# A two-layer transformer trunk on one core: layer 1's modulation without unread columns, the second product in parts of 512 and 256, and the reciprocal square root as a GpSimd power

## The chip, the cores and the metric

The kernel runs on one core of one Trainium2 chip. The metric is the device time of one execution in microseconds (us), as the median of several runs. A core has five engines that work side by side and wait for each other through semaphores: TensorE (PE in the profile, with its weight loads as PEld), VectorE (DVE), ScalarE (ACT), GpSimd (POOL) and SyncE (SP), which issues most DMAs here.

## What is computed

The reference is a trunk of two layers over 512 latent tokens and 256 context tokens, of width 1024. Cut to what matters:

```python
for l in range(2):
    last = l == 1
    m_lat = silu(c) @ w_mod[l] + b_mod[l]          # 6 x 1024
    m_ctx = silu(c_ctx) @ w_mod[l] + b_mod[l]      # 6 x 1024
    sh1, sc1, ga1, sh2, sc2, ga2 = m_lat;  csh1, csc1, cga1, csh2, csc2, cga2 = m_ctx
    h_lat = rmsnorm(x_lat, norm1_g[l]) * (1 + sc1) + sh1
    h_ctx = rmsnorm(x_ctx, norm1_g[l]) * (1 + csc1) + csh1
    z_lat = h_lat @ w_in[l]                        # q, k, v, u, g
    z_ctx = h_ctx @ w_in[l]                        # in the last layer: k and v alone
    # q and k: rmsnorm per head, rotary;  attention over context and latent keys
    # g: gelu, layernorm per group of 128, mixed over 128 positions, times gelu(u)
    x_lat = x_lat + ga1 * (concat(attn_lat, gm_lat) @ w_out[l])
    x_lat = x_lat + ga2 * (relu(modulate(rmsnorm(x_lat), sh2, sc2) @ w_ff1[l]) ** 2 @ w_ff2[l])
    if not last:
        # the same for x_ctx with cga1, csh2, csc2, cga2
return x_lat
```

In the last layer the context gives keys and values and nothing more. Of the context's modulation it needs csh1 and csc1; cga1, csh2, csc2 and cga2 have no reader there.

## The kernel before, in words

Everything is float32. Each product is made of three matmuls on rounded halves: weights and activations are split into a high part `hi` (ScalarE, L207) and a rest `lo` (L208, VectorE or GpSimd), and hi*hi, hi*lo and lo*hi are added up in PSUM through `mm` (L203). A weight block of 128x1024 comes by DMA into `raw`, is split into a ring of four slots, and its slot is released when its last matmul is issued. Activations lie with the channels on the partitions: `X` holds 768 columns, latent tokens in 0 to 511 and context tokens in 512 to 767.

The order of instructions is set in two steps. The kernel's text is written by a planner (`Flow`) with a virtual clock: each matmul adds its cost (L204), and pieces of work are deferred by fixed delays (`PAR`) or drawn from "fillers". Then a scheduler orders each engine's instructions by priority and by its own model of their cost. In layer 0's feed-forward, chunks 0 to 6, VectorE and ScalarE keep the order of the text (`FM0`, L1052); elsewhere, past the start of the program, every engine is ordered by the scheduler. At run time each engine goes through its queue in order, so an instruction that waits holds up all behind it.

**The modulation.** For layer 0 it runs on TensorE (`mod_chunk`). For layer 1, `mod_wide` (L353) runs during layer 0's feed-forward on the engines that have time: 12 blocks j of 512 columns, 8 rows k each. For each k and each of the two conditions (0 latent, 1 context), ScalarE multiplies the weights by one value of silu (L371 for k = 0, L374 for the others) and GpSimd adds the product to `acc` (L375). VectorE then transposes and sums (L386, L387), PE makes a small product (L392), and `mod_store` (L395) adds the bias. The blocks are, two by two, sh1, sc1, ga1, sh2, sc2, ga2. The function yields nine times per block, and the feed-forward draws one step at a time through `more()` (L1013).

**The feed-forward.** `ff1` (L992) makes one tile of 128 hidden channels for all 768 columns, in two parts of 384 (`DENSE`, L538), and `relu2` (L957) squares it in four instructions (L960, L965, L966, L967). Every four tiles form a chunk, and the second product `proj4` (L792, called at L1040) adds a chunk's part to `X`: for 8 output tiles m and for the parts in `passes`, 12 matmuls and then `gate` (L785), which does X = X + ga2 * product (L790). A gate that crosses column 512 is cut there in two, since the two sides have different factors. The second product writes to double banks of PSUM (`pa`, two of them, a part in each half); for every third tile to one bank of `pb` and one of `pt`. In chunk 7 the parts of layer 0 are 512 and 256 in two separate passes already; layer 1 has only the 512 latent columns.

**The reciprocal square root.** `rsqrt` (L280) is a guess from the bits of the number (L283) and two refining steps (L286 to L293): nine small VectorE instructions. It is used by
- `Norm.sums` (L447): twice in layer 0's first norm, twice for each other norm; 4 or 2 columns. The norms of layer 1 are its first (at the end of layer 0's feed-forward) and its second. `diag` (L456) and a broadcast matmul (L460) follow.
- `qk` (L613), once per bank of queries (8 columns) or keys (4 columns). The result is multiplied in at L614, in layer 1 on GpSimd, which also does the sum before it at L608; then come the split (L619, L620) and the transposes on PE (`turn`, L632).
- `sink_g` (L725), once per bank of the gate, 4 columns; VectorE's L727 follows.

In layer 1's attention, `attn_tile` makes a score tile in one of two `pa` buffers; VectorE takes the row maximum (L831), ScalarE the exponential (L834).

Of the kernel before, what the change touches and what calls it, by code (L numbers as in the profile page):

```python
# [8 lines left out]
F32 = mybir.dt.float32  # L9
# [151 lines left out]
def trunk(ctx: ExitStack, tc: tile.TileContext, xT, pk1, pk2, rope, wsT, w_mod, w_tok, w_u, w_out, w_ff1, w_ff2, outT):  # L161
# [115 lines left out]
        state["freed"] += n  # L277
        fl.defer(PAR["REL"], settle)

    def rsqrt(v, n):  # L280

        yi = small(n, I32)
        vec.tensor_scalar(yi, v.bitcast(I32), -0.5, 1595932665.0, op0=ALU.mult, op1=ALU.add)  # L283
        y = yi.bitcast(F32)
        t, r = small(n), small(n)
        vec.tensor_tensor(out=t, in0=y, in1=y, op=ALU.mult)  # L286
        vec.scalar_tensor_tensor(out=t, in0=t, scalar=-0.703952253, in1=v, op0=ALU.mult, op1=ALU.mult)
        vec.scalar_tensor_tensor(out=y, in0=t, scalar=1.681914091, in1=y, op0=ALU.add, op1=ALU.mult)
        vec.tensor_tensor(out=t, in0=y, in1=y, op=ALU.mult)
        vec.tensor_tensor(out=r, in0=t, in1=v, op=ALU.mult)  # L290
        vec.tensor_scalar(t, r, 0.375, -1.25, op0=ALU.mult, op1=ALU.add)
        vec.tensor_tensor(out=t, in0=t, in1=r, op=ALU.mult)
        vec.scalar_tensor_tensor(out=y, in0=t, scalar=1.875, in1=y, op0=ALU.add, op1=ALU.mult)  # L293
        return y
# [5 lines left out]
    ident = P1("ident")  # L300
    ones = const.tile([128, 128], F32, name="ones")
    pool_e.memset(ones, 1.0)
    X = [unit(f"X{i}", [128, 2, T], F32) for i in range(4)]
    for i in range(4):
        nc.sync.dma_start(X[i][:, :, 0:SEQ], xT[i][:, :, 0:SEQ])
# [47 lines left out]
    def mod_wide(l):  # L353

        raw = tk([128, 2, 512], F32)

        def load(i):
            j, k = divmod(i, KT)
            if j < 12:
                (nc.gpsimd if PAR["MQ"] else nc.sync).dma_start(raw[:, k % 2, :], w_mod[l, j, k // 2][:, (k % 2) * 512:(k % 2) * 512 + 512])  # L360
        load(0)
        for j in range(12):
            acc = unit("C1", [128, 2, 512], F32)
            for k in range(KT):
                w = raw[:, k % 2, :]
                load(j * KT + k + 1)
                for cond in range(2):
                    a, s = acc[:, cond, :], sc[:, k, cond:cond + 1]
                    if cond in PAR["MP"]:
                        if k == 0:  # L370
                            act.activation(a, w, AF.Copy, scale=s)  # L371
                        else:
                            p = tsm([128, 512])
                            act.activation(p, w, AF.Copy, scale=s)  # L374
                            pool_e.tensor_tensor(out=a, in0=a, in1=p, op=ALU.add)  # L375
                    elif k == 0:
                        vec.tensor_scalar_mul(a, w, s)
                    else:
                        vec.scalar_tensor_tensor(out=a, in0=w, scalar=s, in1=a, op0=ALU.mult, op1=ALU.add)
                if k not in PAR["YK"]:  # L380
                    yield

            part = small(32).rearrange("p (c b) -> p c b", c=2)
            for cond in range(2):
                tr = tsm([128, 512])
                vec.transpose(tr, acc[:, cond, :])  # L386
                vec.tensor_reduce(out=part[:, cond, :], in_=tr.rearrange("p (b i) -> p b i", i=32), axis=AX.X, op=ALU.add)  # L387
                if cond in PAR["YC"]:
                    yield
            p4 = pt((128, 2, 4))  # L390
            for a in range(4):
                pe.matmul(p4[a * 32:a * 32 + 32], P1("sel"), part.rearrange("p c (m a) -> p c m a", a=4)[:, :, :, a], start=True, stop=True)  # L392
            mod_store(l, j, p4.rearrange("p b a -> p a b"))

    def mod_store(l, j, src):  # L395
        b0 = PK1["bmod"][0] + l * 48 + j * 4
        vec.tensor_tensor(out=modT[l][:, j * 4:j * 4 + 4, :], in0=src, in1=c1[:, b0:b0 + 4].unsqueeze(2).broadcast_to([128, 4, 2]), op=ALU.add)
        if j // 2 in (1, 4):
            w, k0 = (0 if j // 2 == 1 else 1), (j % 2) * 4
            g0 = PK1["ng"][0] + (l * 2 + w) * 8 + k0  # L400
            vec.scalar_tensor_tensor(out=Amod[l][w][:, k0:k0 + 4, :], in0=modT[l][:, j * 4:j * 4 + 4, :], scalar=1.0,
                                     in1=c1[:, g0:g0 + 4].unsqueeze(2).broadcast_to([128, 4, 2]), op0=ALU.add, op1=ALU.mult)

    cx = kv0 = None

# [12 lines left out]
    class Norm:  # L418
# [17 lines left out]
        def sums(self, *others):  # L436

            every = (self,) + others
            ps = pt()
            o = 0  # L440
            for a in every:
                for t in range(a.n // 128):
                    pe.matmul(ps[:, o:o + 1], a.acc[:, t * 128:(t + 1) * 128], ones[:, 0:1], start=True, stop=True)
                    o += 1
            v = small(o)
            vec.tensor_scalar(v, ps[:, 0:o], 1.0 / D, EPS, op0=ALU.mult, op1=ALU.add)
            r = rsqrt(v, o)  # L447
            o = 0
            for a in every:
                a.diag(r[:, o:o + a.n // 128])  # L450
                o += a.n // 128
# [130 lines left out]
    def layer(l, h, nxt, K, kv=None, kv0=0):  # L582
# [11 lines left out]
        def qk(ps4, tp, nh, which):  # L594

            sq = tsm([128, 2, nh, 64])
            act.activation(sq, ps4, AF.Square)
            ss = small(2 * nh)
            vec.tensor_reduce(out=ss.rearrange("p (a b) -> p a b", b=nh), in_=sq, axis=AX.X, op=ALU.add)
            t1 = tw([128, 2, nh, 64])  # L600
            if tp < 2:
                bcast = lambda a: a.unsqueeze(2).broadcast_to([128, 2, nh, a.shape[-1]])
                vec.tensor_tensor(out=t1, in0=ps4, in1=bcast(G[:, which, 0, tp * 2:tp * 2 + 2, :]), op=ALU.mult)
                t2 = tsm([128, 2, nh, 64])
                for hf in range(2):
                    o, i = slice(hf * 32, hf * 32 + 32), slice(32 - hf * 32, 64 - hf * 32)
                    vec.tensor_tensor(out=t2[:, :, :, o], in0=ps4[:, :, :, i], in1=bcast(G[:, which, 1, tp * 2:tp * 2 + 2, o]), op=ALU.mult)
                (pool_e if l in PAR['R1'] else vec).tensor_tensor(out=t1, in0=t1, in1=t2, op=ALU.add)  # L608
            else:
                g = P2(("qg", "kg")[which]).unsqueeze(1).unsqueeze(1).broadcast_to([128, 2, nh, 64])  # L610
                vec.tensor_tensor(out=t1, in0=ps4, in1=g, op=ALU.mult)
            vec.tensor_scalar(ss, ss, 1.0 / HD, EPS, op0=ALU.mult, op1=ALU.add)
            r = rsqrt(ss, 2 * nh)  # L613
            (pool_e if l in PAR['R2'] else vec).tensor_tensor(out=t1, in0=t1, in1=r.rearrange("p (a b) -> p a b", b=nh).unsqueeze(3).broadcast_to([128, 2, nh, 64]), op=ALU.mult)  # L614
            return t1

# [98 lines left out]
        def sink_g(gp):  # L715
            def f(tp, ps):
# [5 lines left out]
                    vec.bn_aggr(out=mv[:, i, :], in_=st[:, i, :])  # L722
                ve = small(4)
                vec.tensor_scalar(ve, mv[:, :, 1], 4 * EPS, None, op0=ALU.add)
                r = rsqrt(ve, 4)  # L725
                for i in range(4):
                    (pool_e if l in PAR['VG'] else vec).tensor_scalar(v[:, i * 128:i * 128 + 128], v[:, i * 128:i * 128 + 128], mv[:, i, 0:1], r[:, i:i + 1], op0=ALU.subtract, op1=ALU.mult)  # L727
                if len(mixes) > 1:
# [289 lines left out]
        def steady(chs):  # L1018
            for ch in chs:
                if ch < 7:  # L1020
                    ff1(ch * 4 + 4)
                    more()
                R = [H.pop(ch * 4 + kk) for kk in range(4)]
                end = ch == 7
                passes, post = [list(dense)], None
                if end and last:
                    post = lambda m, off: nc.sync.dma_start(outT[m], xk(m)[:, 0:SEQ])
                elif end:
                    more(96)
                    n1 = {p[0]: Norm(1, 0, *p) for p in ((0, 512, 0), (512, 256, 1))}  # L1030
                    passes = [[(0, 512)], [(512, 256)]]

                    def post(m, off):
                        nr = n1[off]
                        nr.step(m)
                        if m == 7:
                            if not nxt:
                                nxt.extend(unit(f"A{k}", [128, 2, T]) for k in range(8))
                            nr.finish_later(nxt, None if off == 0 else PAR["NC"])
                for n, _ in enumerate(proj4(("ff2", l, ch), R, 5, passes, "b" if end else "a", post)):  # L1040
                    fl.tick()
                    if n % 2 == 1 and not end:
                        more()
                if not end:
                    for i in range(1, 4):
                        ff1(ch * 4 + 4 + i)
                        more()
# [121 lines left out]
```

## Time and profile before

| | |
|---|---|
| median of 3 runs | 1515.79 us (1515.77 to 1517.52) |
| profiled execution | 1516.59 us |
| its span, first to last instruction | 1514.8 us |
| PE busy | 1463.9 us, 8804 matmuls |
| VectorE busy | 959.7 us, 1874 instructions |
| ScalarE busy | 682.4 us, 1142 instructions |
| GpSimd busy | 403.5 us, 362 instructions |
| mean granted TensorE clock | 0.995 |

How to read the lines that follow. A stretch (a row of the view by windows) gives start and end in us from the span's start, its length, then for PE, PEld, DVE, ACT and POOL the busy time and the number of instructions, then the granted TensorE clock (1.00 is full), the DMA share and GB/s. A group of instructions gives line, engine, operation, output <- inputs, shapes and count, then the total busy time in us and the mean in ns of one, then the idle time before them and what ended it. A timeline row gives start, length, engine, line and operation. A waits row gives who waited for whom: total, times, longest. A row of the chain gives start, length and what, in the chain of work that ended last. L207 is line 207 of the kernel.

Layer 0's attention and projections lie before about 345 us, its feed-forward between 370 and 890, layer 1's projections between 925 and 1040, its attention until 1145, its feed-forward from 1172 to the end.

### The profile page before, as it was taken

How to read it: one execution, taken by the hardware profiler on the slowest of the kernel's cores; microseconds unless marked ns; L12 is line 12 of the kernel's file. 1: busy time of each engine (PE TensorE's matmuls, PEld its weight loads, DVE VectorE, ACT ScalarE, POOL GpSimd, SP SyncE). 2: the span in 40 equal slices, each digit the busy share in tenths (PEclk: the TensorE clock that was granted, in tenths of full speed). 3: DMA queues.
4: the chain of work that ended last, by engine and by line, in shares of the span. 5: the costliest groups of instructions: out<-in, count | busy, mean ns of one | idle time of the engine just before them, and what ended most of it. 6: DMA issues, size and time to landing. Idle time of an engine off the chain costs nothing.

```text
span 1514.8 us, 22788 instructions
## 1 busy us (share of the span) xinstructions
PE 1463.9 (97%) x8804; PEld 1316.3 (87%) x8804; DVE 959.7 (63%) x1874; ACT 682.4 (45%) x1142; POOL 403.5 (27%) x362
## 2 busy tenths in 40 slices
PE   6999899999999999999999999998999999999998
PEld 2899687787899999999999988996899888888887
DVE  5877967787755455555555548888887644444443
ACT  3542455674445454544545334535784333322221
POOL 0112421312054555554545513044212000000000
PEclk9999999999999999999999999999999999999999
DMA  9221344401234333343434311321001323333332
GB/s 362 66 71 55 118 177 156 138 1 42 74 105 132 112 112 125 112 125 98 134 103 127 107 45 56 98 70 56 29 1 56 112 98 98 98 97 97 96 95 76
DMA packets 49948, 148.83 MB, mean 98 GB/s; under 512 B 5424, under 2 KB 6832, under 8 KB 49840
## 3 DMA queue, kind: packets, MB, share of 16 engines
q1 hardware_dynamic: 49264, 146.46, 30.2%
q8 instruction: 69, 1.13, 0.3%
q10 hardware_dynamic: 576, 0.92, 0.2%
q14 instruction: 39, 0.32, 0.1%
HBM read 145.26 MB, written 2.10 MB: 97 GB/s over the span
## 4 chain that ended last, share of the span: by engine, by line
PE 79%; DVE 12%; ACT 3%; DMA 3%; issue 1%; POOL 0%; SPq 0%; ACTq 0%; DVEq 0%; POOLq 0%
PE pa L203 51%; PE pb L203 20%; PE pt L203 3%; PE pt L850 3%; DVE lo L208 1%; PE pb L332 1%; ACT hi L207 1%; DMA raw<-in_w_tok 1%; DMA B<-in_w_mod 1%; DMA A<-in_w_mod 1%; DVE m L283 1%; DVE B L967 1%; DVE m L831 1%; ACT w L834 1%; DVE A L853 1%
## 5 line engine op out<-in xcount | busy, mean ns | idle before, releaser
L203 PE MATMUL pa<-A,hi 128*128 128x384 f32 (+2 forms) x1696 | 449.1, 347 | 1.9 <-ACT w L960 0.6
L207 ACT CAST hi<-raw 128x1024 fp32r<-128x1024 f32 x171 | 179.5, 1050 | 408.9 <-PE pa L203 325.9
L208 DVE TENSOR_TENSOR lo<-raw,hi 128x1024 fp32r<-128x1024 f32 x155 | 203.3, 1312 | 216.5 <-ACT hi L207 213.1
L203 PEld LDWEIGHTS pa<-A,hi 128*128 128x128 f32 x1696 | 304.7, 188 | 26.0 <-ACT w L960 1.8
L375 POOL TENSOR_TENSOR C<-C,s 128x512 f32<-128x512 f32 x168 | 240.4, 1462 | 244.7 <-ACT s L374 244.7
L203 PE MATMUL pa<-A,lo 128*128 128x384 f32 (+2 forms) x848 | 293.6, 347 | 1.1 <-DVE lo L208 1.1
L203 PE MATMUL pa<-B,hi 128*128 128x384 f32 (+1 forms) x900 | 246.5, 356 | 4.4 <-DVE X L790 4.4
L203 PEld LDWEIGHTS pa<-B,hi 128*128 128x128 f32 x900 | 162.9, 188 | 21.6 <-DVE X L790 9.4
L790 DVE SCALAR_TENSOR_TENSOR X<-pa,modT,X 128x384 f32<-128x384 f32 (+1 forms) x168 | 88.0, 547 | 141.9 <-PE pa L203 141.7
L203 PEld LDWEIGHTS pa<-A,lo 128*128 128x128 f32 x848 | 159.3, 188 | 12.3 <-DVE lo L208 1.5
L203 PE MATMUL pa<-B,lo 128*128 128x384 f32 (+1 forms) x450 | 158.1, 353 | 0.0
L203 PE MATMUL pb<-B,hi 128*128 128x256 f32 (+2 forms) x600 | 152.8, 341 | 0.4 <-DVE X L790 0.4
L374 ACT ACTIVATE s<-k,silu 128x512 f32<-128x512 f32 x168 | 114.3, 716 | 47.1 <-DMA k<-in_w_mod 27.6
L203 PE MATMUL pb<-hi,A 128*128 128x256 f32 x672 | 126.2, 285 | 0.0
L203 PEld LDWEIGHTS pb<-B,hi 128*128 128x128 f32 x600 | 103.9, 189 | 11.4 <-DVE X L790 1.0
L790 DVE SCALAR_TENSOR_TENSOR X<-pb,modT,X 128x512 f32<-128x512 f32 (+3 forms) x116 | 69.0, 602 | 69.0 <-PE pb L203 68.8
L203 PEld LDWEIGHTS pb<-hi,A 128*128 128x128 f32 x672 | 106.1, 191 | 0.2 <-issue 0.2
L203 PE MATMUL pb<-B,lo 128*128 128x256 f32 (+2 forms) x300 | 101.6, 339 | 0.0
L203 PE MATMUL pb<-lo,A 128*128 128x256 f32 x336 | 95.3, 284 | 0.0
L203 PEld LDWEIGHTS pa<-B,lo 128*128 128x128 f32 x450 | 84.4, 188 | 5.9
L434 POOL TENSOR_TENSOR acc<-acc,s 128x256 f32<-128x256 f32 (+1 forms) x43 | 47.0, 1092 | 138.7 <-ACT s L432 138.2
L834 ACT ACTIVATE w<-pa,m 128x768 f32<-128x768 f32 (+1 forms) x80 | 65.7, 821 | 38.2 <-DVE m L831 29.8
(171 smaller groups left out, 2321.9 us busy)
## 6 DMA issues: line engine op xcount, KB each, us to landing
raw<-in_w_ff SPq DMA_DIRECT2D x128, 512.0 KB, 3.5
k<-in_w_mod SPq DMA_DIRECT2D x96, 256.0 KB, 2.9
raw<-in_w_tok SPq DMA_DIRECT2D x19, 512.0 KB, 3.6
raw<-in_w_out SPq DMA_DIRECT2D x16, 512.0 KB, 3.5
lo<-in_w_mod SPq DMA_DIRECT2D x16, 512.0 KB, 4.5
hi<-in_w_mod SPq DMA_DIRECT2D x16, 512.0 KB, 3.7
A<-in_w_mod SPq DMA_DIRECT2D x8, 512.0 KB, 10.0
raw<-in_w_u SPq DMA_DIRECT2D x8, 512.0 KB, 3.6
```

What stands on the lines that cost most here:

```text
L203: pe.matmul(out, a, b, start=start, stop=stop)
L207: act.copy(hi, src)
L208: (eng or vec).tensor_tensor(out=lo, in0=src, in1=hi.bitcast(F32), op=ALU.subtract)
L283: vec.tensor_scalar(yi, v.bitcast(I32), -0.5, 1595932665.0, op0=ALU.mult, op1=ALU.add)
L332: pe.matmul(ps[q:q + 32, :], S32[:, k, :], ws_[k2 // 2][:, k2 % 2 * 512:(k2 % 2 + 1) * 512], start=k < ns, stop=k >= KT - ns)
L374: act.activation(p, w, AF.Copy, scale=s)
L375: pool_e.tensor_tensor(out=a, in0=a, in1=p, op=ALU.add)
L434: eng.tensor_tensor(out=self.acc, in0=self.acc, in1=sq, op=ALU.add)
L790: vec.scalar_tensor_tensor(out=xs, in0=src[:, s - off:e - off], scalar=modT[l][:, i * 8 + m, cond:cond + 1], in1=xs, op0=ALU.mult, op1=ALU ...
L831: vec.tensor_reduce(out=nmx, in_=ps[:, 0:nk], axis=AX.X, op=ALU.max, negate=True)
L834: act.activation(p, ps[:, 0:nk], AF.Exp, bias=nmx, accum_out=sm)
L850: pe.transpose(tp_[:, (kt - k0) * 128:(kt - k0) * 128 + 128], p[:, kt * 128:kt * 128 + 128], ident)
```

## The change

Three things, independent of each other.

1. `mod_wide`: for blocks j = 4 to 11 of layer 1 the context condition is left out, from ScalarE's products to the last store. One more `yield` keeps the number of steps per block at nine.
2. `steady`: the second product of layer 0, chunks 0 to 6, goes over the parts (0, 512) and (512, 256) in one pass, in place of (0, 384) and (384, 384). `ff1` keeps its parts of 384.
3. `rsqrt`: in layer 1 the nine VectorE instructions become one GpSimd instruction that raises the number to the power -0.5, with the exponents in a constant tile of 8 columns that GpSimd fills at the start. Layer 0 keeps the nine.

The diff, cut to its core:

```diff
-    def rsqrt(v, n):
-
+    def rsqrt(v, n, l=0):
+
+        if l:
+            y = small(n)
+            pool_e.tensor_tensor(out=y, in0=v, in1=mhalf[:, 0:n], op=ALU.pow)
+            return y
         yi = small(n, I32)
...
+    mhalf = const.tile([128, 8], F32, name="mhalf")
+    pool_e.memset(mhalf, -0.5)
...
         for j in range(12):
+            conds = range(2 if j < 4 else 1)
             acc = unit("C1", [128, 2, 512], F32)
...
-                for cond in range(2):
+                for cond in conds:
...
+            nc_ = len(conds)
             part = small(32).rearrange("p (c b) -> p c b", c=2)
-            for cond in range(2):
+            for cond in conds:
...
-                pe.matmul(p4[a * 32:a * 32 + 32], P1("sel"), part.rearrange("p c (m a) -> p c m a", a=4)[:, :, :, a], start=True, stop=True)
-            mod_store(l, j, p4.rearrange("p b a -> p a b"))
+                pe.matmul(p4[a * 32:a * 32 + 32, 0:nc_], P1("sel"), part.rearrange("p c (m a) -> p c m a", a=4)[:, 0:nc_, :, a], start=True, stop=True)
+            mod_store(l, j, p4[:, 0:nc_].rearrange("p b a -> p a b"), nc_)
+            if nc_ == 1:
+                yield
...
-            r = rsqrt(v, o)
+            r = rsqrt(v, o, self.l)
...
-            r = rsqrt(ss, 2 * nh)
+            r = rsqrt(ss, 2 * nh, l)
...
-                r = rsqrt(ve, 4)
+                r = rsqrt(ve, 4, l)
...
-                passes, post = [list(dense)], None
+                passes, post = [list(dense) if last else [(0, SEQ), (SEQ, CTX)]], None
```

`mod_store` takes the number of conditions and writes and reads only those columns.

More of the change, by code (lines that the diff above doesn't have):

```diff
@@ L391, in mod_wide, with mod_store @@
             for a in range(4):
-                pe.matmul(p4[a * 32:a * 32 + 32], P1("sel"), part.rearrange("p c (m a) -> p c m a", a=4)[:, :, :, a], start=True, stop=True)
-            mod_store(l, j, p4.rearrange("p b a -> p a b"))
-    def mod_store(l, j, src):
+                pe.matmul(p4[a * 32:a * 32 + 32, 0:nc_], P1("sel"), part.rearrange("p c (m a) -> p c m a", a=4)[:, 0:nc_, :, a], start=True, stop=True)
+            mod_store(l, j, p4[:, 0:nc_].rearrange("p b a -> p a b"), nc_)
+            if nc_ == 1:
+                yield
+    def mod_store(l, j, src, nc_=2):
         b0 = PK1["bmod"][0] + l * 48 + j * 4
-        vec.tensor_tensor(out=modT[l][:, j * 4:j * 4 + 4, :], in0=src, in1=c1[:, b0:b0 + 4].unsqueeze(2).broadcast_to([128, 4, 2]), op=ALU.add)
+        vec.tensor_tensor(out=modT[l][:, j * 4:j * 4 + 4, 0:nc_], in0=src, in1=c1[:, b0:b0 + 4].unsqueeze(2).broadcast_to([128, 4, nc_]), op=ALU.add)
         if j // 2 in (1, 4):
@@ L400, in mod_store @@
             g0 = PK1["ng"][0] + (l * 2 + w) * 8 + k0
-            vec.scalar_tensor_tensor(out=Amod[l][w][:, k0:k0 + 4, :], in0=modT[l][:, j * 4:j * 4 + 4, :], scalar=1.0,
-                                     in1=c1[:, g0:g0 + 4].unsqueeze(2).broadcast_to([128, 4, 2]), op0=ALU.add, op1=ALU.mult)
+            vec.scalar_tensor_tensor(out=Amod[l][w][:, k0:k0 + 4, 0:nc_], in0=modT[l][:, j * 4:j * 4 + 4, 0:nc_], scalar=1.0,
+                                     in1=c1[:, g0:g0 + 4].unsqueeze(2).broadcast_to([128, 4, nc_]), op0=ALU.add, op1=ALU.mult)
     cx = kv0 = None
```

## The prediction

> **What bounds the kernel now.** I read the busy table first, then the busy time by stretches, then the waits and the timelines inside the stretches where TensorE is not full.
>
> ```profile
> PE 1463.9 (97%) x8804; PEld 1316.3 (87%) x8804; DVE 959.7 (63%) x1874; ACT 682.4 (45%) x1142; POOL 403.5 (27%) x362
> ```
>
> TensorE (PE) has work 97% of the span. So a step pays only if it makes matmuls shorter or takes away some of the remaining idle time. The stretches tell where that idle time lies (columns: busy time and count of PE, weight loads, VectorE, ScalarE, GpSimd; then the granted clock).
>
> ```profile
> 370.00:878.00 508.00, 502.84 (x2916) 487.83 (x2915) 285.05 (x400) 241.70 (x330) 245.11 (x171) 1.00 0.36 112
> 878.00:985.00 107.00, 105.90 (x668) 95.48 (x667) 77.76 (x196) 47.97 (x79) 18.25 (x17) 1.00 0.21 65
> 985.00:1040.00 55.00, 47.98 (x364) 45.04 (x363) 49.58 (x127) 20.35 (x32) 27.70 (x18) 0.99 0.22 68
> 1145.00:1172.00 27.00, 25.36 (x196) 23.87 (x196) 23.46 (x61) 13.57 (x29) 6.65 (x6) 1.00 0.27 79
> ```
>
> The first row is layer 0's feed-forward, with the second product and layer 1's modulation in it: PE idles 508.00 - 502.84 = 5.2 us. The second is the turn to layer 1 and most of its input projections: 1.1 us idle. The third is the end of those projections and the first attention scores: 55.00 - 47.98 = 7.0 us idle, with VectorE (DVE) busy 90% of it. The fourth is layer 1's second norm: 1.6 us. The change touches these four and nothing else, so idle time of 14.9 us is nearly all that is to be had.
>
> **Part 1, layer 1's modulation.** For blocks j = 4 to 11 the context column goes. Per block that is one scaled copy and 7 scaled products on ScalarE, 7 additions on GpSimd, one transpose and one reduction on VectorE; over 8 blocks 64, 56 and 16 instructions.
>
> ```profile
> L375 POOL TENSOR_TENSOR C<-C,s 128x512 f32<-128x512 f32 x168 | 240.4, 1462 | 244.7 <-ACT s L374 244.7
> L374 ACT ACTIVATE s<-k,silu 128x512 f32<-128x512 f32 x168 | 114.3, 716 | 47.1 <-DMA k<-in_w_mod 27.6
> ```
>
> GpSimd loses 56 x 1.462 = 82 us, ScalarE 64 x 0.716 = 46 us. The loads stay, and so do the nine steps per block (seven rows, one transpose, one closing step), so everything else is issued where it was. All of it lies in the first stretch beside a PE that is 99% busy, where GpSimd was itself waiting 244.7 us for ScalarE: its direct worth is 0. One indirect effect is visible at the start of each second product:
>
> ```profile
> 557.90 1.92 DVE L967 TENSOR_TENSOR B<-w,B 128x768 fp32r<-128x768 f32 x1
> 559.74 0.61 DVE L790 SCALAR_TENSOR_TENSOR X<-pa,modT,X 128x384 f32<-128x384 f32 x1
> ```
>
> ```profile
> L967 DVE TENSOR_TENSOR B<-w,B 128x768 fp32r<-128x768 f32 x24 | 36.6, 1527 | 0.8
> PE pa L203 <- DVE X L790: 4.4, 5, 1.3
> ```
>
> PE waits for the first gated addition L790 (five times, 4.4 us in all), which stands in VectorE's queue behind a subtraction that took 1.92 us here and 1.527 on average. Halved GpSimd work should catch it less often. Bounds 0 and -1.0 us; I take -0.5.
>
> **Part 2, the second product in parts 512 and 256.** Layer 0, chunks 0 to 6, 8 tiles each: 56 tiles, 24 matmuls each, as before. Three rows of the chain, twelve matmuls each, with 384, 512 and 256 columns:
>
> ```profile
> 442.19 2.08 PE pt L203 x12
> 1195.08 2.72 PE pb L203 x12
> 299.37 1.43 PE pb L203 x12
> ```
>
> Before: 2 x 2.08 = 4.16 us a tile; after: 2.72 + 1.43 = 4.15. Over 56 tiles that is -0.6 us, the rounding of the rows. I call it 0. The gated additions change, because the boundary at column 512 no longer cuts a part in two:
>
> ```profile
> L790 DVE SCALAR_TENSOR_TENSOR X<-pa,modT,X 128x384 f32<-128x384 f32 x42 | 25.7, 613 | 13.1 <-PE pa L203 12.9
> L790 DVE SCALAR_TENSOR_TENSOR X<-pa,modT,X 128x128 f32<-128x128 f32 x42 | 14.7, 351 | 83.6 <-PE pa L203 83.6
> L790 DVE SCALAR_TENSOR_TENSOR X<-pa,modT,X 128x256 f32<-128x256 f32 x42 | 19.9, 475 | 0.0
> L790 DVE SCALAR_TENSOR_TENSOR X<-pa,modT,X 128x512 f32<-128x512 f32 x42 | 31.5, 750 | 45.2 <-PE pa L203 45.2
> ```
>
> Before 613 + 351 + 475 = 1439 ns a tile, after 750 + 475 = 1225: 56 x 0.214 = 12 us less on VectorE, which has half of this stretch free, so none of it counts. What counts is the wait at the start of a product. VectorE begins the first L790 when L967 is done, whatever PE does; PE reaches the wait 2.72 - 2.08 = 0.64 us later, and the longer addition ends 0.750 - 0.613 = 0.14 later. Each of the five waits shrinks by 0.5 us: -2.5 us if PE is given as many other matmuls ahead of the wait as now, and if it is given fewer, nothing. A bad order could cost one 0.14 at each of the seven starts, +1.0. I take -2.0.
>
> **Part 3, the power.** There are 34 reciprocal square roots, of nine VectorE instructions each; by the code 15 are layer 1's (four norms, seven query and key banks, four gate banks). Those 135 instructions go, and 15 GpSimd powers on 2 to 8 columns come. The stretch 985 to 1040 holds six of them (count of the first and last of the nine in it):
>
> ```profile
> L283 DVE TENSOR_SCALAR m<-m 128x8 int32<-128x8 int32 (+1 forms) x6 | 6.4, 1067 | 0.1
> L286 DVE TENSOR_TENSOR m<-m 128x8 f32<-128x8 f32 (+1 forms) x6 | 4.3, 708 | 0.2
> L287 DVE SCALAR_TENSOR_TENSOR m<-m,m 128x8 f32<-128x8 f32 (+1 forms) x6 | 3.1, 517 | 0.2
> L293 DVE SCALAR_TENSOR_TENSOR m<-m,m 128x8 f32<-128x8 f32 (+1 forms) x6 | 1.0, 163 | 0.1
> ```
>
> Undisturbed, one takes 0.163 us (the last row, which I take for the five others too). The first three take far more. So VectorE gives 6.4 + 4.3 + 3.1 + 6 x 1.0 = 19.8 us to them in a stretch where it is 90% busy. The timelines of VectorE and of GpSimd show why:
>
> ```profile
> 1030.18 2.32 DVE L283 TENSOR_SCALAR m<-m 128x8 int32<-128x8 int32 x1
> 1032.54 1.22 DVE L286 TENSOR_TENSOR m<-m 128x8 f32<-128x8 f32 x1
> 1033.79 2.27 DVE L287 SCALAR_TENSOR_TENSOR m<-m,m 128x8 f32<-128x8 f32 x1
> 1036.10 0.17 DVE L288 SCALAR_TENSOR_TENSOR m<-m,m 128x8 f32<-128x8 f32 x1
> 1036.58 0.95 DVE L831 TENSOR_REDUCE m<-pa 128x1 f32<-128x768 f32 x1
> ```
>
> ```profile
> 1030.07 2.40 POOL L208 TENSOR_TENSOR lo<-raw,hi 128x1024 fp32r<-128x1024 f32 x1
> 1032.42 1.30 POOL L608 TENSOR_TENSOR w<-w,s 128x512 f32<-128x512 f32 x1
> 1033.67 2.36 POOL L208 TENSOR_TENSOR lo<-raw,hi 128x1024 fp32r<-128x1024 f32 x1
> 1039.16 1.04 POOL L614 TENSOR_TENSOR w<-w,m 128x512 f32<-128x512 f32 x1 [3.12 <-DVE m L836]
> ```
>
> Each of the three tiny instructions ends just after a GpSimd instruction does; VectorE stood still for 5.8 us. Behind them in its queue is L831, the row maximum of the first score tile. ScalarE's exponential waits for that, and PE's third score tile waits for the exponential, since there are two score buffers:
>
> ```profile
> PE pa L203 <- ACT w L834: 4.3, 1, 4.3
> PE pt L632 <- DVE k L620: 1.8, 1, 1.8
> ```
>
> ```profile
> 1038.60:1042.00 3.40, 3.39 (x9) 2.78 (x10) 2.94 (x7) 1.93 (x3) 1.46 (x3) 0.53 0.09 37
> ```
>
> The pause of 4.3 us is followed by 3.4 us at a clock of 0.53, which loses another 3.4 x 0.47 = 1.6 us. [...]
>
> With the nine gone, L831 can follow the scaling L612 at about 1030.2, some six microseconds earlier than now, and the subtraction L620 that made PE wait 1.8 us follows directly on its ScalarE copy. At most 4.3 + 1.6 + 1.8 = 7.7 us come back. Against that stands the power itself, which the trace does not show.
>
> ```profile
> L208 POOL TENSOR_TENSOR lo<-raw,hi 128x1024 fp32r<-128x1024 f32 x16 | 39.6, 2480 | 13.7 <-ACT hi L207 13.6
> L839 POOL COPY rc<-m 128x64 f32<-128x64 f32 x80 | 19.2, 241 | 166.9 <-DVE m L836 154.3 <-PE pt L850 6.8 <-PE pb L871 3.2
> ```
>
> From below it costs 0.24 us, the copy, which handles more columns; from above 2.48, the longest two-input instruction. It is a series of steps per column on few columns, so I take 1.0 us, nearer to the copy. In the stretch six powers make 6 us, and GpSimd has 55.0 - 27.7 = 27.3 free. Queued behind each power are the product L614, or for a gate bank nothing; VectorE waits for gate-bank powers ahead of L727, and a subtraction of 2.4 us may stand ahead of a power in GpSimd's queue. The chain of a query bank gets shorter (nine instructions at 0.163 and their gaps, 1.7 us, become 1.0). Next late are that queue and the tail of VectorE's other work; I give back 1.7 of the 7.7 and take -6.0, with bounds -7.7 and 0.
>
> The four norms hold a similar chain ahead of a broadcast matmul, in stretches with 1.1 + 1.6 = 2.7 us of idle. There the power may stand behind an accumulation on GpSimd. Bounds: -2.7, and +3.0 if each of four powers costs 2.48 against 1.7. I take -0.5.
>
> **Sum.** -0.5 - 2.0 - 6.0 - 0.5 = -9.0 us. The profiled execution took 1516.59 us (its span of 1514.8 and 1.8 around it): 1507.6. The median of the runs shown, 1515.79, is 0.8 lower, which gives 1506.8. The lower bounds of the four terms add to -13.9 (1501.9). As the forecast's upper end I set -3.0 (1512.8), where the moved wait below begins; the upper bounds of the terms together, 0 + 1.0 + 0 + 3.0 = +4.0, belong to the rivals.
>
> **The rivals.** *The wait moves.* Powers of 2 to 4 us, or powers stuck behind GpSimd's 2.4 us subtractions, make PE wait for a turned bank or VectorE for L727. For it: GpSimd's queue is in order, and from 1030 to 1036 it is full. Against: from 1036.04 to 1039.16 it idles. Price: part 3 shrinks to nothing, leaving -2.5 us, 1513.3.
>
> *The power is slow, and GpSimd becomes the bound.* Its free 27.3 us are filled by six powers of 4.5 us; that is the point. At 6 us the stretch needs 27.7 + 36 = 63.7 us of GpSimd against 55 now, +8.7, and the four norms add up to 4 x (6 - 1.7) = 17, of which other matmuls cover perhaps half: with -2.5 from the feed-forward about +15, 1531. VectorE would be stopped as well, as by L208 above, 36 us against the 19.8 freed. [...] Against: no GpSimd row quoted here is longer than 2.5 us, even with 1024 columns.
>
> *The product's parts change nothing.* PE then reaches the wait with fewer other matmuls: part 2 is 0, 1508.8. It lies inside my forecast.
>
> That the change does not do what it says I exclude: no context tile of layer 1 reads the columns dropped.
>
> **How the numbers follow.** Forecast 0.70, the moved wait 0.17, the slow power 0.13. A measurement of this kernel can tell about 0.2%, 3.0 us. The forecast lies beyond that bound, the moved wait within it, the slow power on the other side: 0.70, 0.17, 0.13. The forecast's own range is 1501.9 to 1512.8; for eight in ten I go from 1501.5 to 1517.5, which takes in the moved wait and the mildest slow power.
>
> **What would show it.** Right: in the first stretch the same number of matmuls, PE's wait for L790 near 2 us; between 985 and 1040 no pause of 4 us ahead of a score matmul and no row with half the clock after it; 15 GpSimd powers near 1 us; 19 instead of 34 rows for each of the nine. Wrong: powers beyond 2.5 us, PE waiting for L614's bank or VectorE for a power, or new idle time in layer 1's attention, where the order of the work may come out differently.

## The result, and the profile after

The changed kernel takes 1510.24 us (median of 6 runs, 1507.94 to 1510.43) against 1517.53 us of the kernel before (6 runs, 1515.77 to 1520.26). The ratio is 0.9947, with a 95% interval of 0.9936 to 0.9957: 8 us faster, where 9 were forecast. Behind a ratio, here and below, a difference in us is the ratio applied to the about 1517 us that the kernel before took beside it. The profiled execution took 1510.43 us, its span 1508.6. The stretches of the prediction's first table, now (same columns):

```profile
370.00:878.00 508.00, 503.66 (x2940) 462.68 (x2938) 262.95 (x332) 200.57 (x267) 169.55 (x115) 1.00 0.35 112
878.00:985.00 107.00, 105.56 (x664) 95.36 (x664) 70.44 (x133) 49.05 (x80) 25.75 (x25) 1.00 0.22 69
985.00:1040.00 55.00, 52.60 (x392) 49.06 (x392) 35.74 (x78) 24.64 (x41) 37.93 (x27) 1.00 0.19 59
1145.00:1172.00 27.00, 25.29 (x186) 23.79 (x185) 21.38 (x49) 13.94 (x31) 4.17 (x6) 0.94 0.20 62
```

The third row is the step that counted. PE's idle time there is 55.00 - 52.60 = 2.4 us, down from 7.0; VectorE's busy time fell from 49.6 to 35.7 us, GpSimd's rose from 27.7 to 37.9, and the clock is full. The last row shows something new, a clock of 0.94. PE's longest wait between layer 0's last ReLU and the second norm, and the groups of the new instruction (L284 in this kernel):

```profile
PE pb L203 <- POOL A L791: 2.4, 2, 2.1
```

```profile
L284 POOL TENSOR_TENSOR m<-m,mhalf 128x4 f32<-128x4 f32 x8 | 8.7, 1088 | 39.3 <-DVE m L734 33.3 <-DVE m L456 3.7 <-DVE m L622 2.3
L284 POOL TENSOR_TENSOR m<-m,mhalf 128x8 f32<-128x8 f32 x4 | 7.0, 1760 | 0.0
L284 POOL TENSOR_TENSOR m<-m,mhalf 128x2 f32<-128x2 f32 x3 | 2.1, 711 | 9.1 <-DVE m L456 9.1
```

In layer 0's feed-forward PE still waits for the first gated addition (L800 in this kernel), 3.6 us in four waits where it was 4.4 in five:

```profile
PE pa L203 <- DVE X L800: 3.6, 4, 0.9
```

The waits of 4.3 us (a score matmul for the exponential) and 1.8 us (a transpose for the subtraction) are gone. The one that is now longest stands behind GpSimd's gate subtractions, L781 in the old numbering and L791 in the new. The powers take 0.71, 1.09 and 1.76 us for 2, 4 and 8 columns, (8.7 + 7.0 + 2.1) / 15 = 1.19 on average.

For a comparison free of shifts I cut each trace at four landmarks: layer 0's first and last ReLU, layer 1's last exponential, layer 1's first and last ReLU. Stage lengths in us, from one profile of each kernel:

| kernel | feed-forward 0 | to last exponential | to first ReLU | feed-forward 1 |
|---|---|---|---|---|
| before | 511.6 | 236.5 | 37.2 | 325.5 |
| after | 508.9 | 229.9 | 37.4 | 327.2 |
| part 1 alone (p1_mod) | 509.4 | 236.7 | 36.9 | 325.5 |
| part 2 alone (p2_parts) | 509.6 | 237.5 | 36.9 | 325.6 |
| 256 first (p2_small_first) | 520.6 | 237.3 | 36.9 | 325.6 |
| part 3 alone (p3_power) | 511.6 | 231.0 | 37.4 | 325.7 |
| power in the banks (p3_proj) | 511.4 | 231.0 | 36.9 | 325.6 |
| power in the norms (p3_norm) | 511.1 | 236.5 | 37.5 | 325.7 |
| subtractions on VectorE (wp_vec) | 511.4 | 230.4 | 36.9 | 325.5 |
| all, powers twice (all_twice) | 508.8 | 239.2 | 38.0 | 327.9 |

The change took 2.7 us from the first stage and 6.5 from the second, and gave 0.3 and 1.6 back in the last two. The time ahead of the first ReLU was 1.1 us longer in the profile after. From the unrounded lengths -2.7 - 6.5 + 0.3 + 1.6 = -7.3, and +1.1 makes the -6.2 by which the two spans differ. That first stretch is scatter: in every profile of this document PE, VectorE, ScalarE and GpSimd run the same instructions there in the same order, but for the one GpSimd instruction that fills the exponents, and yet it took 378.3 to 383.0 us. Layer 0's feed-forward, where parts 1 and 2 are left out and its code is as before (p3_power, p3_proj, p3_norm, wp_vec), differs from before by 0.5 us at most.

### The profile page after: what moved, and what is told of

Same layout as the page of the kernel before. It is cut to its first block, busy times and chain, and to the rows that moved or that the text cites. A ratio compares the mean times of both kernels' runs of the same rounds, so it can differ in the third digit from the quotient of the medians.

```text
span 1508.6 us, 22398 instructions
## 1 busy us (share of the span) xinstructions
PE 1461.8 (97%) x8804; PEld 1289.5 (85%) x8804; DVE 908.6 (60%) x1667; ACT 641.0 (42%) x1078; POOL 342.1 (23%) x322
## 4 chain that ended last, share of the span: by engine, by line
PE 83%; DVE 8%; ACT 3%; DMA 2%; POOL 2%; issue 2%; SPq 0%; POOLq 0%; ACTq 0%; DVEq 0%
PE pa L203 52%; PE pb L203 23%; PE pt L860 3%; PE pt L203 2%; PE pb L338 1%; POOL acc L444 1%; DMA raw<-in_w_tok 1%; DMA B<-in_w_mod 1%; PE pt L642 1%; DMA A<-in_w_mod 1%; DVE A L863 1%; DVE m L841 1%; DVE B L977 1%; ACT w L844 1%; PE pb L881 0%
## 5 line engine op out<-in xcount | busy, mean ns | idle before, releaser
L208 DVE TENSOR_TENSOR lo<-raw,hi 128x1024 fp32r<-128x1024 f32 x155 | 196.9, 1270 | 230.7 <-ACT hi L207 227.3
L203 PE MATMUL pa<-B,hi 128*128 128x512 f32 (+1 forms) x900 | 239.8, 355 | 3.6 <-DVE X L800 3.6
L382 POOL TENSOR_TENSOR C<-C,s 128x512 f32<-128x512 f32 x112 | 164.9, 1489 | 314.6 <-ACT s L381 272.6
L203 PEld LDWEIGHTS pa<-B,hi 128*128 128x128 f32 x900 | 158.8, 189 | 31.6 <-DVE X L800 5.9
L800 DVE SCALAR_TENSOR_TENSOR X<-pa,modT,X 128x512 f32<-128x512 f32 x126 | 82.9, 660 | 140.9 <-PE pa L203 140.9
L203 PE MATMUL pb<-B,hi 128*128 128x512 f32 (+1 forms) x600 | 156.9, 350 | 0.9 <-DVE X L800 0.9
L203 PE MATMUL pa<-B,lo 128*128 128x512 f32 (+1 forms) x450 | 157.7, 355 | 0.0
L800 DVE SCALAR_TENSOR_TENSOR X<-pb,modT,X 128x512 f32<-128x512 f32 (+3 forms) x116 | 70.8, 618 | 81.8 <-PE pb L203 81.6
L203 PE MATMUL pb<-B,lo 128*128 128x512 f32 (+1 forms) x300 | 104.5, 348 | 0.0
L381 ACT ACTIVATE s<-k,silu 128x512 f32<-128x512 f32 x112 | 76.9, 715 | 38.8 <-DMA k<-in_w_mod 25.9
L203 PE MATMUL pb<-A,hi 128*128 128x512 f32 (+2 forms) x288 | 81.7, 360 | 2.4 <-POOL A L791 2.4
```

The lines of the kernel that those rows point to most:

```text
L203: pe.matmul(out, a, b, start=start, stop=stop)
L208: (eng or vec).tensor_tensor(out=lo, in0=src, in1=hi.bitcast(F32), op=ALU.subtract)
L800: vec.scalar_tensor_tensor(out=xs, in0=src[:, s - off:e - off], scalar=modT[l][:, i * 8 + m, cond:cond + 1], in1=xs, op0=ALU.mult, op1=ALU ...
```

## Experiments: which part gave what

My theory was the prediction's: part 2 shortens PE's wait at the start of each product, part 1 adds little, and part 3 frees VectorE's queue at the end of the projections. The rivals: the feed-forward's gain is part 1's, or the whole is a lucky order of the work.

**Part 1 alone.** `rsqrt` and the product's parts as before:

```diff
+            conds = range(2 if j < 4 else 1)
...
-                for cond in range(2):
+                for cond in conds:
```

> The first part alone (modulation without the unread columns; products in 384 and 384, nine VectorE instructions everywhere). Of the 6.2 us between the two profiled spans, layer 0's feed-forward (first to last ReLU) gave 2.7. My theory (the gain there is the longer first part of the product): this one gives 0 to -1 us, 1515 to 1517, and the waits for the first gated addition stay at 4 to 5.3 us in all. Rival (halved GpSimd work stops slowing VectorE): all of the 2.7 us, 1513 to 1514.5, with the subtraction after ReLU below its 1527 ns mean.

Ratio 0.9989 (0.9980 to 0.9997), -1.7 us; the feed-forward's stage is 2.1 us shorter. PE's waits for the gated addition (L794 here) in that stage:

```profile
PE pa L203 <- DVE X L794: 2.6, 3, 0.9
PEld pa L203 <- DVE X L794: 7.1, 25, 1.3
```

Three waits instead of five: those at 698 and 767 us, of 1.3 and 0.6 us, are gone. Both signs failed: my theory had 4 to 5.3 us of waits, and the rival's shorter subtraction has a mean of 1484 ns, hardly under 1527. The traces show two different causes. At 698 us the subtraction was caught before: a GpSimd addition that had begun ahead of it ran from 695.26 to 697.08 us, and the subtraction took 1.94 us and ended 0.82 after it. With part 1 alone it took 0.96; first before, then part 1 alone:

```profile
695.96 1.94 DVE L967 TENSOR_TENSOR B<-w,B 128x768 fp32r<-128x768 f32 x1
```

```profile
695.23 0.96 DVE L971 TENSOR_TENSOR B<-w,B 128x768 fp32r<-128x768 f32 x1
```

That is a matter of 0.02 us: here the subtraction began at 695.23 and GpSimd's addition at 695.25, and it was the addition that took longer (2.08 us). In the kernel with all three parts the addition began first, at 695.86, and the subtraction took 1.93 us again. At 767 us the subtraction took 0.96 us in both kernels. What stood between it and the gated addition before was the modulation's own store, in which a tiny instruction (L401, 0.17 us in the median of its eight) took 1.14 us beside a GpSimd addition that ran from 765.51 to 766.81 us; again before, then part 1 alone:

```profile
764.63 0.96 DVE L967 TENSOR_TENSOR B<-w,B 128x768 fp32r<-128x768 f32 x1
765.50 0.16 DVE L397 TENSOR_TENSOR modT<-pt,c 128x8 f32<-128x8 f32 x1
765.70 1.14 DVE L401 SCALAR_TENSOR_TENSOR A<-modT,c 128x8 f32<-128x8 f32 x1
766.76 0.60 DVE L790 SCALAR_TENSOR_TENSOR X<-pa,modT,X 128x384 f32<-128x384 f32 x1
```

```profile
763.29 0.96 DVE L971 TENSOR_TENSOR B<-w,B 128x768 fp32r<-128x768 f32 x1
764.17 0.61 DVE L794 SCALAR_TENSOR_TENSOR X<-pa,modT,X 128x384 f32<-128x384 f32 x1
```

The added `yield` keeps nine steps per block but stands behind the store, so the store is issued one step earlier, here at 757 us. By the traces this wait went because the store moved, and not because GpSimd had less to do.

**Part 2 alone.**

```diff
-                passes, post = [list(dense)], None
+                passes, post = [list(dense) if last else [(0, SEQ), (SEQ, CTX)]], None
```

> The second part alone (512 and 256). My theory: -2 us, 1513.5 to 1515.5, PE's first waits shorter than the 1.0 us of before by 0.5 each. Rival (matmul time equal, order the same): 0, 1515.5 to 1517.5.

Ratio 0.9994 (0.9985 to 1.0002), -0.9 us, not clear of nothing; the stage itself is 1.9 us shorter, as forecast. The second stage of its profile is 1.0 us longer, with 6.8 us at half clock instead of 3.4 (last section). But the waits of its profile contradict my reason. First before, then part 2 alone, in layer 0's feed-forward:

```profile
PEld pa L203 <- DVE X L790: 9.4, 25, 1.6
```

```profile
PE pa L203 <- DVE X L790: 4.2, 5, 1.0
PEld pa L203 <- DVE X L790: 7.0, 7, 1.4
```

The five long waits are there, 4.2 us instead of 4.4. The timeline of VectorE and the chain behind it show one of them:

```profile
558.32 1.93 DVE L967 TENSOR_TENSOR B<-w,B 128x768 fp32r<-128x768 f32 x1
560.17 0.74 DVE L790 SCALAR_TENSOR_TENSOR X<-pa,modT,X 128x512 f32<-128x512 f32 x1
```

```profile
560.97 1.93 PE pa L203 x13
```

VectorE does what it did, and PE starts its second part when L790 is done; ahead of the wait it now has no other tile's matmuls left, since the scheduler gave it fewer. What did go are 18 waits of weight loads: of the 25 before, five are those of the long waits and the others 0.16 to 0.31 us long, and 7 are left in all. The matmuls behind such a wait took longer. Before, twelve of them with and without a first weight load that had waited, here 0.16 us, for a gated addition:

```profile
438.76 2.22 PE pa L203 x12
442.19 2.08 PE pt L203 x12
```

18 times about 0.1 us are the 1.9 us. Summed over the whole stage, the extra spacing of matmuls next to such load waits, the five long waits apart, was 2.8 us before (26 places) and is 0.8 us now (8 places). That a gate of one addition of 475 ns, in place of two of 351 and 475, is done before the weight load asks for it is the likely reason; the trace does not prove it.

**Part 2 the other way round.**

```diff
-                passes, post = [list(dense)], None
+                passes, post = [list(dense) if last else [(SEQ, CTX), (0, SEQ)]], None
```

> The second part with 256 ahead of 512. If the wait at the start of a product is set by VectorE's subtraction and shrinks with a longer first part (my theory), a first part of 1.43 us in place of 2.08 makes each of the five waits longer by 0.65 us: +3 us, 1518.5 to 1520.5. Rival (the scheduler fills in other matmuls whatever the first part is): as 512 first, within 1 us of it.

Ratio 1.0063 (1.0050 to 1.0076), +9.6 us, and 9.0 of them in the feed-forward's stage.

```profile
PE pa L203 <- DVE X L790: 9.3, 15, 0.9
PEld pa L203 <- DVE X L790: 9.5, 13, 1.3
```

The order of the parts matters, against the rival, and three times as much as I said, but not by my mechanism. The waits at the five starts did not grow by 0.65 us each: they are 0.95, 0.76, 0.76, 0.77 and 0.56 us, 3.8 in all where 4.4 stood before. The loss is in ten other waits, 5.5 us. Six of them (3.6 us) are at a product's end, where the first matmuls of the next feed-forward tile now wait for the longer addition. So the first part's length does not set the wait at the start in either order.

**Part 3 alone.** Every power of the change, products in 384 and both conditions kept.

```diff
+        if l:
+            y = small(n)
+            pool_e.tensor_tensor(out=y, in0=v, in1=mhalf[:, 0:n], op=ALU.pow)
+            return y
```

> The third part alone (powers in layer 1). My theory: -6 to -6.5 us, 1509.5 to 1511.5, all of it between layer 0's last ReLU and layer 1's last exponential; powers of 1.2 us mean. Rival (the order of the work came out luckily with all three together): under -4 us or over -9 us.

Ratio 0.9966 (0.9954 to 0.9978), -5.2 us; the second stage is 5.5 us shorter, the first unchanged. That is neither under 4 nor over 9, as the rival had it, and the three parts alone add up to -7.8 where the whole gave -8.0. The order of the work still has a share. By stages the parts do not add up: 4.1 us against 2.7 in the first, 4.2 against 6.5 in the second. And in this kernel the 3.4 us at half clock are still in the second stage, behind a wait of 2.14 us for GpSimd's gate subtraction, where the whole has none.

**The power in the banks alone, and in the norms alone.** The first leaves `r = rsqrt(v, o)` in the norms, the second leaves it in `qk` and `sink_g`:

```diff
-            r = rsqrt(v, o, self.l)
+            r = rsqrt(v, o)
```

```diff
-            r = rsqrt(ss, 2 * nh, l)
+            r = rsqrt(ss, 2 * nh)
...
-                r = rsqrt(ve, 4, l)
+                r = rsqrt(ve, 4)
```

> Before, with the power in layer 1's eleven query, key and gate banks only; its four norms keep the nine VectorE instructions. My theory (the gain is VectorE's queue at the end of the projections): -4 to -5 us of the third part's 5.2, 1511.5 to 1513. Rival (the norms, whose first broadcast came 2.7 us earlier after layer 0's last ReLU, give half of it): -2.5 us, about 1514.

> Before, with the power in layer 1's four norms only. My theory: -0.5 us, 1515.5 to 1517, the 2.7 us by which the first broadcast comes earlier are given back by the first scores. Rival: they last, -2.5 us, about 1514.

In the banks: 0.9950 (0.9936 to 0.9964), -7.6 us. In the norms: 1.0011 (1.0001 to 1.0020), +1.7. So all of part 3's gain lies in the banks. The norms' second stage is 236.5 as before: the first broadcast came earlier and the scores did not. Behind the second norm 0.3 us are lost. The difference between p3_proj and p3_power is not settled: their intervals overlap, and their second stages are the same 231.0 us.

## Experiments: why the nine instructions were dear

**The nine kept, GpSimd's subtractions moved.** Nothing of the change; the eight subtractions of layer 1's output weights go to VectorE:

```diff
-       "FM0": 'DA', "FM1": '', "FC": 7, "MP": [0, 1], "YC": [0, 1], "YK": [0], "RM": {}, "WP": ['out1', 'out0'],
+       "FM0": 'DA', "FM1": '', "FC": 7, "MP": [0, 1], "YC": [0, 1], "YK": [0], "RM": {}, "WP": ['out0'],
```

> Before, nine VectorE instructions everywhere, but the eight subtractions of layer 1's output weights go from GpSimd (2.4 us each) to VectorE (1.2 us each). My theory (VectorE stands still while GpSimd runs a two-input instruction, so it is GpSimd's work that makes the nine long): the mean of the first of the nine between 985 and 1040 us falls from 1067 ns to below 600, and the time between layer 0's last ReLU and layer 1's last exponential falls by 1 to 4 us although VectorE has 6 us more to do. Rival (only the amount of VectorE work counts): it grows by 2 to 5 us, 1518 to 1521.

Ratio 0.9955 (0.9942 to 0.9968), -6.8 us, with five more subtractions on VectorE between 985 and 1040:

```profile
L208 DVE TENSOR_TENSOR lo<-raw,hi 128x1024 fp32r<-128x1024 f32 x7 | 8.5, 1217 | 0.0
L283 DVE TENSOR_SCALAR m<-m 128x8 int32<-128x8 int32 (+1 forms) x6 | 5.4, 894 | 0.1
L287 DVE SCALAR_TENSOR_TENSOR m<-m,m 128x8 f32<-128x8 f32 (+1 forms) x6 | 1.0, 163 | 0.2
L286 DVE TENSOR_TENSOR m<-m 128x8 f32<-128x8 f32 (+1 forms) x6 | 1.0, 158 | 0.1
```

L286 and L287 fell from 708 and 517 ns to 158 and 163, and the same code in the same place lost 4.3 + 3.1 - 2.0 = 5.4 us of VectorE time because GpSimd's subtractions were no longer beside it. L283 stayed at 894 where I expected below 600: it still meets the sum L608 on GpSimd. Two of its six, at 1020.48 and 1029.33 us, took 1.22 and 1.25 us beside sums that ran from 1020.38 to 1021.67 and from 1028.20 to 1030.55. The waits:

```profile
PE pt L632 <- DVE k L620: 1.3, 1, 1.3
PE pa L203 <- ACT w L834: 0.9, 1, 0.9
```

The pause of 4.3 us is down to 0.9, and no half clock follows in this trace. The amount of VectorE work, the rival, would have made it slower. So the nine were not dear as nine instructions; most of their time, 19.8 us before where 54 instructions of 0.163 would be 8.8, was spent standing behind GpSimd.

**Every power twice**, the first one's result unread, on top of all three parts:

```diff
-            y = small(n)
+            y0, y = small(n), small(n)
+            pool_e.tensor_tensor(out=y0, in0=v, in1=mhalf[:, 0:n], op=ALU.pow)
             pool_e.tensor_tensor(out=y, in0=v, in1=mhalf[:, 0:n], op=ALU.pow)
```

> All three parts, each power preceded by a second one whose result nobody reads: 15 more powers of 1.2 us. If the power's length is on the path in every bank, the six of the last stretch cost 7 to 9 us: 1517 to 1519. My theory (GpSimd has room there and most banks have other matmuls in front): +2 to +4 us over all three parts, 1512 to 1514.5. Rival (the power is wholly covered): 0 to +1, 1510 to 1511.5.

Ratio 1.0017 (1.0007 to 1.0026). Against all three parts that is 1.0017 / 0.9947 = 1.0070, +10.6 us for 8.8 + 6.5 + 2.1 = 17.4 us more of powers (its groups of the added line), and the second stage grew by 9.3 us. My theory of 2 to 4 us falls, and even the case of every bank, 7 to 9 us, was too low. Some 3.4 us of it are the clock's: this profile has two stretches of 3.4 us at half clock in the second stage, where the changed kernel's has none. New or longer waits stand there:

```profile
PE pb L203 <- DVE s L618: 1.9, 1, 1.9
PE pt L471 <- DVE w L467: 1.8, 2, 1.1
PE pt L643 <- DVE k L631: 1.8, 1, 1.8
```

The room in GpSimd's queue (55.0 - 37.9 = 17 us in the stretch) did not help. My reading is that the wait is one of latency: bank after bank, and norm after norm, somebody stands behind the power. The waits fit it, but no run separates it from the work of other instructions that the longer queue shifts.

## Experiments: what is late next, and a better version

All four have parts 1 and 2. The first has the power in the banks only; the second no power and the subtractions on VectorE; the third both; the fourth the power in the banks and layer 1's gate subtractions on VectorE:

```diff
-                (pool_e if g > 1 else vec).tensor_tensor(out=gm[:, 1, 0:TQ], in0=src, in1=gm[:, 0, 0:TQ].bitcast(F32), op=ALU.subtract)
+                (pool_e if g > 1 and not last else vec).tensor_tensor(out=gm[:, 1, 0:TQ], in0=src, in1=gm[:, 0, 0:TQ].bitcast(F32), op=ALU.subtract)
```

> All three parts, but the four norms of layer 1 keep the nine VectorE instructions. The parts alone gave -2.7 us (one and two together, in layer 0's feed-forward) and -7.6 us (power in the banks alone): -9 to -10.5 us, 1506.5 to 1508, better than all three parts by 1 to 2.5 us. Rival (the norm's loss is the shifted half-clock stretch and not the power): as all three parts, -8 us.

> Parts one and two, no power at all, and the subtractions of layer 1's output weights on VectorE. If freeing VectorE from GpSimd's long instructions is worth what the power is worth, -2.7 - 6.8 = -9.5 us, 1506.5 to 1508.5. Rival (parts one and two need a lighter VectorE later on): -7 us or less.

> Parts one and two, the power in the banks alone, and the subtractions on VectorE. My theory (both remove the same pause of 4.3 us and the half clock behind it): only 0 to 2 us better than either alone, 1505 to 1508. Rival (two separate gains): -2.7 - 7.6 - 6.8 = -17 us, about 1500.

> Parts one and two, the power in the banks alone, and layer 1's two gate subtractions that GpSimd does go to VectorE. They stand behind the powers and are what PE waits for longest now (2.2 us). My theory: that wait goes, 1 to 2.5 us better than without this edit, 1504.5 to 1507. Rival (VectorE has the same queue again): no better, or the pause ahead of the third score tile returns, +2 us or more.

| kernel | median | ratio (interval) | feed-forward 0 | to last exponential |
|---|---|---|---|---|
| all_no_norm | 1509.09 | 0.9947 (0.9934 to 0.9959) | 509.1 | 231.6 |
| mod_parts_wp_vec | 1506.58 | 0.9928 (0.9916 to 0.9941) | 508.2 | 230.4 |
| all_no_norm_wp_vec | 1511.44 | 0.9960 (0.9947 to 0.9973) | 509.1 | 232.7 |
| all_no_norm_gm_vec | 1508.29 | 0.9939 (0.9927 to 0.9950) | 509.1 | 228.0 |

Leaving the norms out changed nothing against all three parts, as the rival said. The traces agree with its reason: from the first ReLU of layer 0 to the last of layer 1 the two profiles differ by 0.3 us, and each has one stretch of 3.4 us at half clock, at the second norm with all three parts and ahead of the scores without the norms' powers. Moving the subtractions is worth as much as the power: without any power the kernel is at 0.9928, -10.9 us, near the -9.5 expected. So the two gains are not separate (that rival would be near 1500). Together they are worse than the subtractions moved without a power, which I had not expected; against the power without them the intervals overlap. In its profile this wait grew from 2.4 us, and 3.4 us at half clock follow it:

```profile
PE pb L203 <- POOL A L791: 3.2, 1, 3.2
```

With that wait taken away (the fourth) the second stage is the shortest of all, 228.0, 1.9 us under all three parts. Its median does not show it. The time ahead of the first ReLU was 383.0 us in its profile, against 378.9 before and 381.9 in the second kernel's; the instructions there are the same, and 20.5 us of it were at half clock, against 10.2 and 17.1. Which of the second and fourth is better stays open, as their intervals overlap. The second beats the kernel before beyond doubt; its lead over the change, whose interval it overlaps from 0.9936 to 0.9941, is likely but not shown.

## Why the prediction was right, point by point

- **Sum and time.** -9.0 forecast, -8.0 measured by the ratio; 1506.8 against 1510.24, inside the range. Half of those 3.4 us is the start of the sum: the kernel before took 1515.79 us in the runs that the forecast began from and 1517.53 beside the changed one. Several of the reasons were wrong and made up for each other, and that is luck: parts 1 and 2 were to give 2.5 us and gave 2.7, hardly any of it by the steps named.
- **Part 1, -0.5 with a bound of -1.0.** -2.1 us in its stage, alone. The effect named, L967 caught by GpSimd at a product's start, gave one wait of 1.3 us, by a start 0.02 us earlier; in the changed kernel it is caught there again. The other wait, 0.6 us, had no caught L967: the reading that all five stood behind one was wrong. It went because the store moved by one step, so "everything else is issued where it was" failed too.
- **Part 2, -2.0.** The number held (-1.9), the step failed: "each of the five waits shrinks by 0.5 us" did not happen, by the clause that I had put beside it (PE given fewer other matmuls). The gain came from short waits of weight loads, which I had not priced. Most of that is not idle time of PE: with part 2 alone its busy time in the stage fell from 506.4 to 504.7 us, outside the 14.9 us of idle time that were to be nearly all there was to be had. The sign "PE's wait for L790 near 2 us" failed as well: the changed kernel waits 3.6 us, in four waits. Equal matmul time and VectorE time off the path were right. Together with part 1 it gives 2.7 and not 4.0, since the 1.3 us of part 1 are missing.
- **Part 3, -6.0 in the projections.** Right in place and mechanism: the 4.3 and 1.8 us waits went, and 2.4 us came back as a wait for GpSimd's queue where I gave back 1.7. Part 3 alone shortened the stage by 5.5, all parts by 6.5. The term that failed is the clock, 1.6 us of the 7.7. The pause of 4.3 us went and half clock still came: in part 3 alone it stays in this stage, behind a wait of 2.14 us, and with all parts it came at the second norm, where it costs the 1.6 us again (below). That the size held without it is partly luck.
- **Norms, -0.5.** Nothing in the stage, +0.3 behind it.
- **Power, 1.0 us.** 1.19 measured. That it was "nearer to the copy" held for 2 columns; for 8 it took 1.76. The series of steps per column was an assumption; the runs show lengths alone, 0.71, 1.09 and 1.76 us for 2, 4 and 8 columns. My point at which the slow power decides, 4.5 us from GpSimd's free time, was far too high: doubling it already ate the gain, clock included. The rival's price asked when the queue is full and not who waits for each power; by the waits above I think that is why it was wrong. Nor does a power stop all of VectorE: in the changed kernel, while the power at 1022.52 us ran for 2.10, VectorE's L609, at 1023.64, took its usual 0.67 us.

## What to carry to other kernels

A tiny instruction that takes ten times its usual length (here 2.32 us where 0.163 is usual) is a sign to look at the neighbouring engine's timeline at the same moment; taking the neighbour's work away was worth as much here as taking the tiny instructions away, and the same pause can be removed only once. Before moving a step to an idle engine ask not how much room that engine has but who waits for each result; doubling the step is a cheap test. And a split of the work before a buffer's reuse is worth trying in both orders: here the order decided between -2 and +9 us in the stage.

## What the runs showed of the hardware

GpSimd's instructions were longer beside VectorE's too: in the kernel with the subtractions on VectorE, GpSimd's sum L608 took 2.35 us, against 1.29 at 1020.38, beside VectorE's subtraction at 1028.19. In the two cases told here in which GpSimd's instruction took longer, this one and the one at 695.25 us with part 1 alone, VectorE's had begun first, by 0.01 and 0.02 us.

```profile
1028.19 1.21 DVE L208 TENSOR_TENSOR lo<-raw,hi 128x1024 fp32r<-128x1024 f32 x1
```

```profile
1020.38 1.29 POOL L608 TENSOR_TENSOR w<-w,s 128x512 f32<-128x512 f32 x1
1028.20 2.35 POOL L608 TENSOR_TENSOR w<-w,s 128x512 f32<-128x512 f32 x1
```

Half clock also came behind pauses much shorter than the 4.3 us of the kernel before. In the kernel with all parts but the norms' powers (all_no_norm), a wait of 2.15 us and one of 0.28 us stood ahead of it. In the changed kernel the same wait, 2.14 us, passed at full clock; half clock came at the second norm, behind pauses of 1.0 and 0.4 us, and cost the 1.6 us by which feed-forward 1 is longer. All_no_norm first, then the changed kernel's second norm:

```profile
1026.04 0.50 PE L203 MATMUL pb<-A,hi 128*128 128x512 f32 x1 [2.15 <-POOL A L791]
```

```profile
1028.30:1031.70 3.40, 3.40 (x11) 2.76 (x10) 2.74 (x4) 0.57 (x1) 3.40 (x3) 0.56 0.28 82
```

```profile
1159.20:1162.60 3.40, 3.15 (x12) 2.97 (x13) 2.42 (x7) 1.31 (x3) 0.00 (x0) 0.50 0.16 66
```

Whether a pause is followed by half clock can be counted over all fourteen profiles, between 1010 and 1050 us. All six pauses of PE of 3.2 us or more were; of the eleven between 1.7 and 2.2 us, six were. Each stretch lasts 3.4 us or a multiple, and 3.4 us at a clock of 0.5 lose about 1.7 us, which is as much as some of the edits above are worth. The time at half clock (the stretches in which the trace has a granted clock of 0.5), in us, by stage:

| kernel | ahead of the first ReLU | to last exponential | feed-forward 1 |
|---|---|---|---|
| before | 10.2 | 3.4 | 0 |
| after | 13.7 | 0 | 3.4 |
| p1_mod | 6.8 | 6.8 | 0 |
| p2_parts | 13.7 | 6.8 | 0 |
| p2_small_first | 13.7 | 6.8 | 0 |
| p3_power | 13.7 | 3.4 | 0 |
| p3_proj | 13.7 | 3.4 | 0 |
| p3_norm | 17.1 | 3.4 | 0 |
| wp_vec | 10.2 | 0 | 0 |
| all_twice | 13.7 | 6.8 | 3.4 |
| all_no_norm | 10.2 | 3.4 | 0 |
| mod_parts_wp_vec | 17.1 | 0 | 0 |
| all_no_norm_wp_vec | 13.7 | 3.4 | 0 |
| all_no_norm_gm_vec | 20.5 | 0 | 0 |

So a difference of a us or two between two single profiles in these stages can be one stretch more or less of half clock. Executions of one kernel differ by it too: of the changed kernel's six, the fastest, 1507.94 us, had a mean clock of 0.998, and the three slowest, of 1510.4, had 0.994.
